# Two-layer hybrid trunk on one core: low halves of the activations in a plane of their own, ring slots of low weights at four start offsets

## The chip, the cores and the metric

The kernel runs on one core of a Trainium2 chip. The metric is the device time of one execution in microseconds, lower is better; a result is the median of several runs.

## What is computed

Two layers act on a residual stream x of 256 tokens by 1024 channels, in float32. Cut to what matters for the time:

```python
for l in range(DEPTH):                                   # DEPTH = 2
    mix = hybrid_mixer(x, w_in[l], ...)                  # one input projection, three mixers, merge, output projection
    x = layer_norm(ALPHA * x + mix, ln1_g[l], ln1_b[l])
    ffn = swiglu(x, w_ffn_gate[l], w_ffn_up[l], w_ffn_down[l])   # (silu(x @ w_gate) * (x @ w_up)) @ w_down, hidden 2816
    x = layer_norm(ALPHA * x + ffn, ln2_g[l], ln2_b[l])
```

The mixers are a sliding-window attention, a gated short convolution and a block attention (with 256 tokens, plain causal attention). Each is projected to 1024 channels, weighted by a sigmoid gate and summed. Nearly all arithmetic is the products of x, and of what is made from it, with weight matrices.

## The kernel before, in words

**Products in three parts.** Each float32 operand is split into a high half (rounded to the type `float32r`) and a low half (what the rounding left). A product is three matmuls: high by high, high by low, low by high. They come in trios from two helpers, both through `mm` on line 256, so that nearly all matmuls have that line:

```python
def trio(acc, wh, wl, src, first, last):         # weights stationary, 256 tokens moving
    mm(acc, wh, src[:, 0, :], first, False)
    mm(acc, wh, src[:, 1, :], False, False)
    mm(acc, wl, src[:, 0, :], False, last)
```

`tokens` does the same the other way round: 128 tokens are stationary and 256 or 512 columns of weights move. Of each matmul the weight load of the stationary operand is an instruction of its own (LDWEIGHTS). In a trio the order of stationary operands is wh, wh, wl and of moving ones high, low, high; in `tokens` the stationary ones are high, high, low and the moving ones wh, wl, wh.

**Weights.** The weights stand in DRAM as 140 pieces of 128 partitions by 2048 columns (70 for a layer), in the order of use. SyncE loads a piece into one of 3 `raw` tiles; ScalarE writes its high half `wh` (line 184) and VectorE its low half `wl` (line 185), in two chunks of 1024 columns. The halves go to the pool `wts`, which has four slots for `wh` and four for `wl`. Each slot is 2048 elements, 8192 bytes in a partition. The slots are used in turn, and `drop` frees one when its last matmul is issued. Three pieces of a layer go to other places, the halves of one tile `wA` or `wB`, and do not pass through the ring.

**Activations.** `xx` holds x transposed, as 8 blocks of 128 channels; of each block the 256 high halves come first and then the 256 low halves (index order k, a, s). 48 elements (`AHEAD`, 192 bytes) are left free ahead of it, and a filler tile `rest` of 16 elements brings the sum back to a multiple of 256 bytes. `y`, the results of the three mixers, has the same 48 elements ahead. `mx` (input of the output projection), `hidA` and `hidB` (the FFN's hidden values) have none.

**Stages, and which helper each uses.** For each layer: `whole` (tile `acc`, `trio` on `xx`) for the input projections, among which the attention rounds (`s`, `tp`, `yp`) are interleaved; `cv`, a product with 512 moving columns of weights; `branch` (tile `br`, `trio` on `y`); `merge` (tile `gc`, `trio` on `xx`); `project` (tile `pr`, `tokens` on `mx`, 512 moving columns); `half_pair` (tile `hp`, `tokens` on `xx`, 256 moving columns) for the first FFN pieces, and for the first input projections of each layer; `whole` again (tile `acc`) for the FFN's 18 remaining pieces; `project` on `hidA`, `hidB`, where the last layer has some blocks of 256 columns.

**The order of the work.** A planner (`Plan`) sets, while the program is built, the order on TensorE, VectorE, ScalarE and SyncE from costs that it holds; addresses play no part in it.

**Offsets before.** Start addresses here are bytes within a partition, modulo 256. Each slot of `wh` and `wl` starts at 0, and each stationary or moving block within it is a multiple of 512 bytes further, so all weights stand at 0. All blocks of `xx` and `y`, high and low, stand at 192; `mx`, `hidA` and `hidB` at 0.

Of the kernel before, what the change touches and what calls it, by code (L numbers as in the profile page):

```python
# [10 lines left out]
FR = mybir.dt.float32r  # L11
# [5 lines left out]
P = 128  # L17
D = 1024
S = 256
L = 2  # L20
KD = D // P
# [3 lines left out]
PIECE = 2048  # L25
# [7 lines left out]
LN_EPS = 1e-5  # L33
FAR = 1.0e30
LINE = 64
AHEAD = 48


# [77 lines left out]
def trunk(ctx: ExitStack, tc: tile.TileContext, x, xt, w, sinks, conv, ln, out):  # L116
# [4 lines left out]
    wts = pool("wts", RING)  # L121
    keep = pool("keep", 1)
# [13 lines left out]
    spare, ready, chunks, raw, landed, rawfree = {}, {}, {}, {}, {}, {}  # L136
# [6 lines left out]
    def load(ks=None):  # L143
        j = pos["load"]
        if j >= total:
            return
        pos["load"] += 1
        raw[j] = raws.tile([P, PIECE], FT, name="raw")
        if ks is None:
            for s in cut(j):  # L150
                nc.sync.dma_start(raw[j][:, s], w[j][:, s])
        else:
            a, b = by_k(raw[j]), by_k(w[j])
            for k in ks:
                nc.sync.dma_start(xs[:, k, :], xt[:, k, :])
                nc.sync.dma_start(a[:, :, k, :], b[:, :, k, :])  # L156
        landed[j] = max(landed.get(j - 1, 2.5), rawfree.get(j - RAWS, 0.0) + 2.0) + 3.0
        open_splits()
# [4 lines left out]
    def open_splits():  # L163
        while pos["split"] < pos["load"]:
            j = pos["split"]
            if j in place:
                if place[j] not in spare:
                    return
                t = spare.pop(place[j])
                both = keep.tile([P, 2, PIECE], FR, tag=place[j], name="w" + place[j])  # L170
                ready[j] = both[:, 0, :], both[:, 1, :]
            else:
                if not slots:
                    return
                t = slots.pop(0)
                ready[j] = wts.tile([P, PIECE], FR, name="wh"), wts.tile([P, PIECE], FR, name="wl")
            pos["split"] += 1
            if j:
                split_piece(j, max(t, landed[j]))
# [7 lines left out]
    def split_piece(j, t, n=CHUNK):  # L187
        def last(task):
            rawfree[j] = task.ready
            load()  # L190

        need = T.pe + 5.2 * (j - pos["take"])
        ss = [slice(c, c + n) for c in range(0, PIECE, n)]
        chunks[j] = [T.add(parts(j, s), t - (1.5 if len(cut(j)) > 1 and not i else 0.0), max(need - t, 0.0) + 0.001 * i, last if s.stop == PIECE else None)
                     for i, s in enumerate(ss)]

    def take():
        j = pos["take"]
        pos["take"] += 1
        T.run()  # L200
        T.finish(*chunks.pop(j))
        return j

    def drop(j):
        if j in place:
            if j % PER_LAYER == N_IN + N_BR + N_OUT:
                spare["B"] = T.pe
        else:
            slots.append(T.pe)
        del ready[j]  # L210
        open_splits()
# [90 lines left out]
        users.append(t)  # L302
        return t

    xx = keep.tile([P, AHEAD + KD * 2 * S], FR, name="xx")
    xx = xx[:, AHEAD:].rearrange("p (k a s) -> p k a s", k=KD, a=2)
    xk = [xx[:, k] for k in range(KD)]
    rest = keep.tile([P, LINE - AHEAD], FT, name="rest")
    nc.gpsimd.memset(rest, 0.0)
# [292 lines left out]
    def mixer_tiles():  # L602
        mix = keep.tile([P, 18 * S + 4 * (S + 2) + 56], FT, tag="mix", name="mix")
        aq, ak, av, cq, ck, cv = [
            mix[:, lo * S:hi * S].rearrange("p (k s) -> p k s", k=k)
            for lo, hi, k in ((0, 4, 4), (4, 5, 1), (5, 6, 2), (6, 10, 4), (10, 14, 4), (14, 18, 2))]
        return aq, ak[:, 0, :], av, cq, ck, cv, mix[:, 18 * S:18 * S + 4 * (S + 2)].rearrange("p (k s) -> p k s", k=4)
# [26 lines left out]
    for l in range(L):  # L634
        aq, ak, av, cq, ck, cv, up = tiles = mix or mixer_tiles()
        y = keep.tile([P, AHEAD + 12 * 2 * S], FR, tag="A", name="y")
        y = y[:, AHEAD:].rearrange("p (b k a s) -> p b k a s", b=3, k=4, a=2)
        nc.gpsimd.memset(up[:, :, 0:2], 0.0)
# [39 lines left out]
        for n in range(2):  # L678
            j = take()
# [50 lines left out]
        if l == 0:  # L730
            rest = keep.tile([P, LINE - AHEAD], FT, name="rest2")
            nc.gpsimd.memset(rest, 0.0)
# [70 lines left out]
        merge()  # L803
        spare["A"] = spare["B"] = T.pe
        open_splits()

        hid, last_f = [], {f: [] for f in range(NF)}
# [125 lines left out]
```

## Time and profile before

| | us |
|---|---|
| median of 3 runs | 862.95 (859.62 to 865.4) |
| the profiled execution | 860.16 |
| its span, first to last instruction | 858.4 |
| granted TensorE clock, mean over the span | 0.997 |
| TensorE matmuls busy | 844.8 (98%) |
| VectorE busy | 583.5 (68%) |
| ScalarE busy | 456.3 (53%) |

The span is 1.8 us shorter than the profiled execution's own time. A duration of a matmul in the profile is that of one instruction with its fill and drain, and successive matmuls overlap; how fast they follow one another is read from their starts.

### The profile page before, as it was taken

The page shows a single profiled execution, that of the slowest core. Times are in us where ns is not written, and L with a number is a line of the kernel's source. Part 1 is how long each engine was busy: PE and PEld are TensorE (multiplying, and loading weights), DVE is VectorE, ACT ScalarE, POOL GpSimd, SP SyncE. Part 2 cuts the span into 40 slices and gives each one's busy share as a digit, 9 for nine tenths or more (in the row PEclk, how much of TensorE's full clock was granted, in tenths as well). Part 3 has the DMA queues.
Part 4 walks back from the last instruction along what each step waited for, and adds up shares of the span by engine and source line. Part 5 has one row for each costly group of instructions (what it writes and reads, how often), then busy time and mean ns, then how long its engine had stood idle before and what let it go on. Part 6 is the DMA issues. An engine that isn't in the chain of part 4 may idle for free.

```text
span 858.4 us, 15516 instructions
## 1 busy us (share of the span) xinstructions
PE 844.8 (98%) x6374; PEld 797.3 (93%) x6374; DVE 583.5 (68%) x977; ACT 456.3 (53%) x809; POOL 51.4 (6%) x81
## 2 busy tenths in 40 slices
PE   7999999999999999999999999999999999999996
PEld 7989999999899999988899899999997999999885
DVE  5678888567976666545656798876689575666435
ACT  6667577745535445434337757776564254444320
POOL 2003400000100000000000034000000000000000
PEclk9999999999999999999999999999999999999998
DMA  8754535365755555556337352544557465555511
GB/s 300 289 195 150 187 108 186 140 216 176 265 197 180 174 187 197 196 189 238 119 116 255 116 196 99 186 138 169 196 197 254 139 245 187 173 185 193 196 50 49
DMA packets 24822, 155.16 MB, mean 181 GB/s; under 512 B 2704, under 2 KB 4528, under 8 KB 7344
## 3 DMA queue, kind: packets, MB, share of 16 engines
q1 hardware_dynamic: 23536, 149.96, 49.9%
q0 software_dynamic: 1216, 4.22, 1.5%
q8 instruction: 50, 0.82, 0.4%
q14 instruction: 20, 0.16, 0.1%
HBM read 153.11 MB, written 1.05 MB: 180 GB/s over the span
## 4 chain that ended last, share of the span: by engine, by line
PE 96%; DMA 2%; DVE 1%; ACT 0%; issue 0%; SPq 0%; POOLq 0%; POOL 0%; DVEq 0%
PE acc L256 47%; PE pr L256 17%; PE hp L256 9%; PE br L256 8%; PE gc L256 5%; PE s L256 3%; PE cv L256 3%; PE tp L271 2%; DMA gb<-ln 1%; PE yp L474 1%; DMA xs<-xt 1%; PE yp L476 0%; DVE xtok L502 0%; DVE wA L185 0%; SPq L156 0%
## 5 line engine op out<-in xcount | busy, mean ns | idle before, releaser
L256 PE MATMUL acc<-xx,wh 128*128 128x256 f32 x2304 | 408.9, 282 | 5.6 <-ACT wh L276 5.6
L185 DVE TENSOR_TENSOR wl<-raw,wh 128x1024 fp32r<-128x1024 f32 x266 | 321.9, 1228 | 123.2 <-ACT wh L184 122.3
L184 ACT ACTIVATE wh<-raw 128x1024 fp32r<-128x1024 f32 x266 | 273.5, 1054 | 188.5 <-PE acc L256 81.6
L256 PEld LDWEIGHTS acc<-xx,wh 128*128 128x128 f32 x2304 | 353.9, 190 | 6.7 <-ACT wh L276 6.2
L256 PE MATMUL acc<-xx,wl 128*128 128x256 f32 x1152 | 323.2, 281 | 0.0
L256 PEld LDWEIGHTS acc<-xx,wl 128*128 128x128 f32 x1152 | 217.7, 189 | 0.2 <-DVE wl L277 0.2
L256 PE MATMUL hp<-wh,xx 128*128 128x256 f32 x384 | 70.5, 281 | 0.0
L283 DVE TENSOR_TENSOR g<-g,acc 128x256 f32<-128x256 f32 x72 | 30.1, 417 | 58.7 <-PE acc L256 58.7
L256 PE MATMUL br<-y,wh 128*128 128x256 f32 x384 | 67.9, 281 | 0.0
L256 PE MATMUL pr<-wh,hidA 128*128 128x512 f32 (+1 forms) x216 | 60.8, 366 | 0.0
L256 PEld LDWEIGHTS hp<-wh,xx 128*128 128x128 f32 x384 | 59.5, 188 | 0.0
L256 PEld LDWEIGHTS br<-y,wh 128*128 128x128 f32 x384 | 59.0, 190 | 0.0
L256 PE MATMUL br<-y,wl 128*128 128x256 f32 x192 | 54.0, 281 | 0.0
L256 PE MATMUL hp<-wl,xx 128*128 128x256 f32 x192 | 53.5, 279 | 0.0
L256 PE MATMUL gc<-xx,wh 128*128 128x256 f32 x256 | 45.3, 281 | 0.0
L256 PEld LDWEIGHTS pr<-wh,hidA 128*128 128x128 f32 x216 | 39.1, 189 | 6.7
L256 PE MATMUL pr<-wh,hidB 128*128 128x512 f32 (+1 forms) x144 | 41.8, 366 | 0.0
L256 PE MATMUL pr<-wl,hidA 128*128 128x512 f32 (+1 forms) x108 | 39.6, 366 | 0.0
L256 PEld LDWEIGHTS gc<-xx,wh 128*128 128x128 f32 x256 | 39.3, 190 | 0.0
L429 ACT ACTIVATE prob<-prob,st 128x128 f32<-128x128 f32 x32 | 12.6, 395 | 46.3 <-DVE st L426 23.3
L256 PEld LDWEIGHTS hp<-wl,xx 128*128 128x128 f32 x192 | 36.1, 188 | 0.0
L256 PEld LDWEIGHTS br<-y,wl 128*128 128x128 f32 x192 | 36.0, 188 | 0.0
(130 smaller groups left out, 982.0 us busy)
## 6 DMA issues: line engine op xcount, KB each, us to landing
raw<-w SPq DMA_DIRECT2D x136, 1024.0 KB, 4.9
gb<-ln POOLq DMA_DIRECT2D x8, 512.0 KB, 5.9
raw<-w SPq DMA_DIRECT2D x6, 512.0 KB, 6.5
xtok<-x SPq DMA_DIRECT2D x2, 512.0 KB, 6.3
xs<-xt SPq DMA_DIRECT2D x3, 256.0 KB, 5.4
raw<-w SPq DMA_DIRECT2D x3, 256.0 KB, 5.5
out<-xtok SPq DMA_DIRECT2D x3, 256.0 KB, 2.0
xs<-xt SPq DMA_DIRECT2D x2, 128.0 KB, 2.5
```

The lines of the kernel that those rows point to most:

```text
L184: return [act(n) + (lambda: nc.scalar.activation(wh[:, s], raw[j][:, s], AF.Copy),), dve(n) + (lambda: nc.vector.tensor_sub(wl[:, s], raw[ ...
L185: dve(n) + (lambda: nc.vector.tensor_sub(wl[:, s], raw[j][:, s], wh[:, s].bitcast(FT)),)]
L256: nc.tensor.matmul(acc, a, b, start=start, stop=stop)
L271: nc.tensor.transpose(tp[:, i, :], src(i), ident)
L283: return [dve(n) + (lambda: nc.vector.tensor_mul(dst, a, b),)]
L429: nc.scalar.activation(t[:, 0, :], t[:, 0, :], AF.Exp, bias=st[:, 2:3], scale=0.125, accum_out=st[:, 4:5])
L474: nc.tensor.matmul(yp[los[a], :], v[:, 0, vsel[a]], pts[a][:, 0:2, :], start=True, stop=False)
```

## The change

`xx` is laid out as two planes: first all high halves (8 blocks of 256), then all low halves. Between the planes 32 elements (`APART`, 128 bytes) are left free, and as many after the second, so that the tile stays a multiple of 256 bytes with `AHEAD` and `rest`. The high halves stay at 192 modulo 256; the low ones stand at 192 + 8192 + 128, which is 64 modulo 256.

Each slot for low weights gets 16 elements more than are used (64 bytes), so that the four slots, which lie one after the other, start at 0, 64, 128 and 192 modulo 256. The slots for high weights, `wA`, `wB`, `y`, `mx` and the hidden values stay where they were modulo 256.

```diff
+APART = 32
...
-                ready[j] = wts.tile([P, PIECE], FR, name="wh"), wts.tile([P, PIECE], FR, name="wl")
+                ready[j] = (wts.tile([P, PIECE], FR, name="wh"),
+                            wts.tile([P, PIECE + 16], FR, name="wl")[:, :PIECE])
...
-    xx = keep.tile([P, AHEAD + KD * 2 * S], FR, name="xx")
-    xx = xx[:, AHEAD:].rearrange("p (k a s) -> p k a s", k=KD, a=2)
+    xx = keep.tile([P, AHEAD + 2 * (KD * S + APART)], FR, name="xx")
+    xx = xx[:, AHEAD:].rearrange("p (a r) -> p a r", a=2)[:, :, :KD * S].rearrange("p a (k s) -> p k a s", k=KD)
```

No instruction is added, removed or moved: each engine has the same instructions with the same waits in the same order. Three splits of `xs` at the start, on ScalarE and VectorE each, now write one run of 512 elements where they wrote two of 256.

## Rows read from the trace of the kernel before

**Rows 1.** The page, part 1: busy us (share) and count of instructions.

```profile
PE 844.8 (98%) x6374; PEld 797.3 (93%) x6374; DVE 583.5 (68%) x977; ACT 456.3 (53%) x809; POOL 51.4 (6%) x81
```

**Rows 2.** The page, part 4: shares of the chain that ended last, by engine.

```profile
PE 96%; DMA 2%; DVE 1%; ACT 0%; issue 0%; SPq 0%; POOLq 0%; POOL 0%; DVEq 0%
```

**Rows 3.** The chain in order of time: start us, us, engine, tile, line, matmuls.

```profile
3.09 4.51 DMA xs<-xt
...
21.22 8.16 PE hp L256 x72
...
76.24 8.18 PE acc L256 x72
...
90.29 8.48 PE acc L256 x72
...
162.61 33.92 PE br L256 x288
196.53 22.61 PE gc L256 x192
...
269.16 98.94 PE acc L256 x840
...
428.99 8.48 PE hp L256 x72
```

**Rows 4.** TensorE in time, slow rhythm: start us, us, engine, line, operation.

```profile
303.86 0.28 PE L256 MATMUL acc<-xx,wl 128*128 128x256 f32 x1
...
303.98 0.40 PE L256 MATMUL acc<-xx,wh 128*128 128x256 f32 x2
...
304.10 0.19 PEld L256 LDWEIGHTS acc<-xx,wl 128*128 128x128 f32 x1
304.22 0.28 PE L256 MATMUL acc<-xx,wl 128*128 128x256 f32 x1
```

**Rows 5.** TensorE in time, last projection, blocks of 256 columns.

```profile
848.75 0.88 PE L256 MATMUL pr<-wB,hidB 128*128 128x256 f32 x6
849.47 0.28 PE L256 MATMUL pr<-wh,hidB 128*128 128x256 f32 x1
```

**Rows 6.** TensorE in time, eight transposes in a row.

```profile
250.28 1.03 PE L271 MATMUL tp<-ident,xtok 128*128 128x128 f32 x8
251.15 0.38 PE L271 MATMUL tp<-ident,gh 128*128 128x128 f32 x2
```

**Rows 7.** TensorE in time, 512 moving columns: the tile cv, then the tile pr.

```profile
50.81 0.39 PE L256 MATMUL cv<-wl,xx 128*128 128x512 f32 x1
...
52.87 0.39 PE L256 MATMUL cv<-wl,xx 128*128 128x512 f32 x1
...
370.25 0.39 PE L256 MATMUL pr<-wl,hidA 128*128 128x512 f32 x1
...
371.61 0.39 PE L256 MATMUL pr<-wl,hidA 128*128 128x512 f32 x1
```

**Rows 8.** Groups by line, different shapes apart: busy us, mean ns, idle before.

```profile
L256 PE MATMUL acc<-xx,wl 128*128 128x256 f32 x1152 | 323.2, 281 | 0.0
L185 DVE TENSOR_TENSOR wl<-raw,wh 128x1024 fp32r<-128x1024 f32 x266 | 321.9, 1228 | 123.2 <-ACT wh L184 122.3
...
L256 PE MATMUL gc<-xx,wl 128*128 128x256 f32 x128 | 36.0, 281 | 0.0
...
L256 PE MATMUL pr<-wl,hidA 128*128 128x512 f32 x84 | 32.8, 390 | 0.0
...
L256 PE MATMUL pr<-wl,hidB 128*128 128x512 f32 x56 | 21.8, 390 | 0.0
...
L256 PE MATMUL pr<-wl,mx 128*128 128x512 f32 x48 | 18.7, 390 | 0.0
```

**Rows 9.** Stretches: us, PE busy (count), granted clock, DMA share, GB/s.

```profile
34.00:40.00 6.00, 6.00 (x55) 1.00 0.86 300
...
285.00:355.00 70.00, 70.00 (x597) 1.00 0.53 185
```

## The prediction

> **What bounds the kernel now.** I read the page first, then the chain, then TensorE's starts. The page shows matmuls busy for 98% of the span [rows 1], and the chain that ended last runs through TensorE for 96% [rows 2], so the time is what its 6,374 matmuls take one after the other. Busy time cannot tell whether they run at their best, since a busy 281 ns [rows 8] is a matmul with its fill and drain. How close they follow shows in the chain, which gives a piece's length and its count of matmuls [rows 3]. The reader is to see that the same work has two paces: 72 matmuls of the tile acc take 8.18 us in one piece (113.6 ns each) and 8.48 us in the next (117.8 ns). The clock does not differ: it is granted in full in a stretch of either kind [rows 9]. In the slow FFN piece of 840 matmuls the mean is 98.94 / 840 = 117.8 ns, so the pace holds for a hundred microseconds.
>
> Adding up the chain's pieces of acc, hp, br and gc by their pace gives 3,624 matmuls at 117 ns and above: in each of the two layers 840 of the FFN, 288 br and 192 gc [rows 3], 2,640 together, and 984 in pieces of 24 to 72, as the hp piece at 428.99 and the acc piece at 90.29. The other 1,416 with 256 columns are at 113 to 114 ns, all in the mixers' part of the two layers; 5,040 in all.
>
> **What addresses have to do with it.** The weight load of the next matmul begins with the matmul now running [rows 4]: the load of wl at 304.10 starts beside the second wh matmul, the one that moves the low activations. So each matmul has a moving operand and a load that read SBUF at the same time. I call their difference of start addresses, moving less stationary, modulo 256 bytes, the offset of the pair. Before, the offset is 192 for all of acc, gc and br and 64 for all of hp. The rows with other offsets:
> - Offset 0, 256 columns (last projection): six matmuls start in 849.47 - 848.75 = 0.72 us, 120.0 ns each [rows 5].
> - Offset 192: 113.6 or 117.8 ns. Offset 64 (hp): 8.16 / 72 = 113.3 or 8.48 / 72 = 117.8 ns [rows 3].
> - Offset 128: only transposes, which move 128 columns: eight in 251.15 - 250.28 = 0.87 us, 108.8 ns each [rows 6]. Half as many moving columns make this a lower bound and not a price.
> - 512 columns: offset 64 (cv) nine in 2.06 us, 229 ns; offset 0 (pr) six in 1.36 us, 227 ns [rows 7].
>
> So the offset is worth some ns for a matmul, but the same offset has two paces, and once a pace is taken it lasts until something interrupts it. Which one is taken after an interruption differs between two attention rounds of the same form (the pieces at 76.24 and 90.29) [rows 3].
>
> **The change, part by part.** It moves no instruction, so only durations and paces can change. The sum is made against the profiled execution's 860.16 us; the median of the runs is 862.95, 2.8 us above it, and the same difference is applied to that.
>
> *The low plane and the low slots.* In a trio two pairs keep their offset of 192 (high activations beside wh). The third, low activations (64) beside wl at 0, 64, 128 or 192, gets 64, 0, 192 or 128 in place of 192, a quarter of the pieces each. What this does to the pace no row shows. Bounds: every one of the 5,040 at 120.0 (3,624 x 2.2 + 1,416 x 6.4 ns = +17.0 us), every one at 108.8 (3,624 x 9.0 + 1,416 x 4.8 ns = -39.4 us). I take the value that the fast pieces show, 113.6, for the stages whose moving operand is `xx` or whose stationary operand is: the slow pace needs three equal pairs in a row for as long as 840 matmuls, and now one in three differs and differs anew with each piece of weights. This is where I choose, and it is the weakest step. For br I take nothing, as `y` does not move. Then 3,624 - 576 = 3,048 matmuls gain 117.8 - 113.6 = 4.2 ns: -12.8 us.
>
> *The quarters that do worse or better.* acc and gc have 1,152 + 128 = 1,280 matmuls with wl, one for each low pair [rows 8], 320 for each slot. The slot at 64 gives offset 0, 120.0 in place of 113.6: 320 x 6.4 ns = +2.0 us. The slot at 192 gives offset 128, taken at the bound of 108.8: 320 x 4.8 = -1.5 us. In hp (offsets of wl moving against low activations) and br the two cancel within 0.4 us. Sum: -12.8 + 2.0 - 1.5 = -12.3 us.
>
> *Projections.* Of pr's matmuls with 512 columns, 84 + 56 + 48 = 188 move low weights of the ring [rows 8], and three quarters of them change offset. Between 227 and 229 ns that is 188 x 0.75 x 2 ns = 0.3 us either way; I take nothing.
>
> *Splits.* VectorE writes wl at other addresses, 266 chunks of 1,228 ns [rows 8]. It has 123 us of waiting for ScalarE before them, so a few ns more in each would be covered. The three longer runs at the start replace as many elements; the start waits for loads (4.51 us in the first piece of the chain) [rows 3]. Both at nothing.
>
> *What comes late next.* With 12 us less on TensorE nothing else is near: VectorE is busy 68%, ScalarE 53% [rows 1], and the FFN moves 185 GB/s where another stretch moved 300 [rows 9].
>
> Forecast: 862.95 - 12.3 = 850.6, said as 851 us.
>
> **A rule against the change.** The rows give 113.6, 117.8 and 120.0 ns to matmuls of one shape, [rows 3, 5], and the first two differ at the same full clock [rows 9]. The Trainium skill, page "TensorE: Matmul & The Clock Gate", section "Step-by-step: what each phase is for", says of the two read ports: "Loading the next tile's weights doesn't steal SBUF read bandwidth from the running matmul." By that rule the offsets mean nothing and the result is 863. The trace does not bear it out, since the matmuls at offset 0 are slower than any at 192; but those belong to another tile, so it is not refuted either, and it stands below as the first rival.
>
> **The rivals.**
> - *Offsets mean nothing* (863). The paces come from elsewhere, and the change touches nothing that counts. For it: the paces change where attention interrupts, with no change of address [rows 3]. Against it: 120.0 at offset 0 [rows 5].
> - *Gains and losses cancel* (859, 855 to 871). The two pairs at 192 keep their pace, and only the third changes. For it: one offset has both paces, so the offset does not decide alone, and with the middle of the two paces, 115.7, for offsets 64 and 192, the four slots have a mean of (115.7 + 120.0 + 115.7 + 108.8) / 4 = 115.1 against 117.8, 2.7 ns on one matmul in three or 5,040 / 3 x 2.7 = 4.5 us. Against it: the slow pace would have to outlive a change of every third pair.
> - *The new offsets bring on the slow pace* (872). A new slot every 48 matmuls is an interruption, and after it the slow pace is taken, as after the round before 90.29. The 1,416 fast matmuls then lose 4.2 ns, +5.9 us; in the quarter with offset 0 the trio as a whole falls to 120.0, 5,040 / 4 x 2.2 = +2.8 us; and the projections lose what cv has over pr, +0.3. Sum +9.0: 872.0. It decides once the 1,416 are lost and one slot drags its trio. For it: at offset 0 every matmul of the row takes 120. Against it: before the interruptions mostly lead into the fast pace (the pieces with 8.18).
> - *More than forecast* (840). br follows as well, all 3,624 gain 4.2 ns (-15.2), and low pairs go to 108.8 in every trio, 5,040 / 3 x 4.8 = -8.1.
>
> **How the numbers follow.** Forecast 0.40, offsets mean nothing 0.10, cancel 0.22, slow pace 0.20, more 0.08. That the change does not do what it says is left out: the sizes of the tiles fix the addresses. Faster by over 1% (under 854.3; 1% is about what a measurement of this kernel tells from no change) takes the forecast and more, 0.48; same 0.32; slower (over 871.6) 0.20. Range: 840 below and the slow rival above with its edge, 838 to 874. The forecast's own range is 845 to 856.
>
> **What would show it.** In the chain after: FFN pieces at 113 to 114 ns a matmul (95.6 us for 840) say the forecast; 98.9 us says nothing moved; over 100 us the slow rival. The pace piece by piece should repeat every four pieces of weights if slots decide. br at 33.9 us for 288 says `y` is untouched. It would be wrong if the pace stayed even over all four slots.

## The result, and the profile after

| | before | after |
|---|---|---|
| median of 20 runs, us | 862.15 (859.62 to 866.96) | 868.91 (866.48 to 873.28) |
| the profiled execution, its span, us | 860.16, 858.4 | 869.29, 867.5 |

The ratio is 1.0085, with a 95% interval of 1.0073 to 1.0098: the change makes the kernel 0.85% slower, 6.8 us. Forecast were 851 us, with a range of 838 to 874. The range holds the result, but the sign of the forecast was wrong.

The page after, parts 1 and 4, beside [rows 1, 2]:

```profile
PE 851.8 (98%) x6374; PEld 801.3 (92%) x6374; DVE 585.6 (68%) x977; ACT 457.0 (53%) x809; POOL 50.9 (6%) x81
PE 95%; DMA 2%; DVE 1%; SPq 1%; issue 0%; ACT 0%; POOLq 0%; POOL 0%; DVEq 0%
```

The counts are the same, and TensorE is still the chain. Matmul busy time rose by 7.0 us; where it was lost the page cannot say. The chain in order of time can. After (start us, us, engine, tile, line, matmuls):

```profile
6.81 7.68 DMA raw<-w
...
22.67 8.51 PE hp L258 x72
...
79.02 8.57 PE acc L258 x72
...
93.56 8.57 PE acc L258 x72
...
167.40 33.11 PE br L258 x288
200.51 22.75 PE gc L258 x192
...
273.51 99.51 PE acc L258 x840
373.02 56.58 PE pr L258 x246
...
434.63 8.39 PE hp L258 x72
...
504.00 8.43 PE acc L258 x72
...
592.42 33.39 PE br L258 x288
...
699.51 99.58 PE acc L258 x840
799.09 61.13 PE pr L258 x330
```

And the chain before at those places that [rows 3] leave out:

```profile
368.10 55.80 PE pr L256 x246
...
583.75 33.92 PE br L256 x288
...
691.20 98.94 PE acc L256 x840
790.14 60.95 PE pr L256 x330
```

The starts of the same stage in both give an account of the 9.1 us between the two profiled executions (the medians lie 6.8 us apart; the execution profiled before was 2 us under its median):

| stretch | lost, us |
|---|---|
| up to the first hp piece (21.22, then 22.67) | 1.45 |
| mixers of the first layer, up to br (162.61, then 167.40: 4.79 - 1.45) | 3.34 |
| br and gc, first layer (33.92 + 22.61, then 33.11 + 22.75) | -0.67 |
| projection and hp, up to the FFN (269.16, then 273.51) | 0.23 |
| FFN, first layer (98.94, then 99.51) | 0.57 |
| projections, up to hp (428.99, then 434.63) | 0.72 |
| mixers of the second layer, up to br (583.75, then 592.42) | 3.03 |
| br to the FFN, second layer (691.20, then 699.51) | -0.36 |
| FFN, second layer (98.94, then 99.58) | 0.64 |
| the rest | 0.18 |

The first row is the landing of the first loads and has nothing to do with the change: in the profiled executions of the kernels below, where the chain has that hp piece, it starts anywhere between 20.98 and 23.35. Of the other 7.7 us, 6.4 are lost in the mixers. There [rows 3] have pieces of 72 in 8.18 and 8.48 us; after, no piece of 72 in acc is under 8.43. The fast pace is gone. br, which the forecast held untouched, gained 0.5 to 0.8 us.

The pace of acc after repeats every four pieces of weights; in time the slots come in the order 128, 0, 192, 64. The clock is granted in full (1.00 from 285 to 355 us). TensorE in time, first layer's FFN, the matmuls with wl, one for each trio: the end of a piece in the slot at 192, then the slot at 64 (start us, us, engine, line, operation):

```profile
307.36 0.29 PE L258 MATMUL acc<-xx,wl 128*128 128x256 f32 x1
...
309.88 0.29 PE L258 MATMUL acc<-xx,wl 128*128 128x256 f32 x1
...
311.30 0.28 PE L258 MATMUL acc<-xx,wl 128*128 128x256 f32 x1
...
313.38 0.28 PE L258 MATMUL acc<-xx,wl 128*128 128x256 f32 x1
```

From 307.36 to 309.88 there are seven trios: 2.52 us / 21 = 120.0 ns a matmul. From 311.30 to 313.38 there are six: 2.08 / 18 = 115.6 ns. The same means over all parts of 24 matmuls of that FFN, split by the pair (mean ns from one start to the next in the trace, without the first six and the last of each part, good to about 1 ns; in brackets the offset of the pair):

| slot | high by wh | low by wh | high by wl | mean |
|---|---|---|---|---|
| 0 | 116.2 (192) | 119.6 (64) | 117.4 (192) | 117.7 |
| 64 | 113.6 (192) | 118.4 (0) | 115.0 (192) | 115.7 |
| 128 | 119.0 (192) | 122.5 (192) | 120.3 (192) | 120.6 |
| 192 | 121.4 (192) | 115.1 (128) | 123.4 (192) | 120.0 |

The reader is to see two things. The low pair's own offset counts for some ns, as forecast. But the first pair, whose addresses modulo 256 are the same in all four rows, takes 113.6 to 121.4 ns: a pair cannot be priced alone. The mean of the four slots is 118.5, above the slow pace of before.

### The profile page after: what moved, and what is told of

Read it like the earlier page. It is cut to its first block, busy times and chain, and to the rows that moved or that the text cites. A ratio compares the mean times of both kernels' runs of the same rounds, so it can differ in the third digit from the quotient of the medians.

```text
span 867.5 us, 15516 instructions
## 1 busy us (share of the span) xinstructions
PE 851.8 (98%) x6374; PEld 801.3 (92%) x6374; DVE 585.6 (68%) x977; ACT 457.0 (53%) x809; POOL 50.9 (6%) x81
## 4 chain that ended last, share of the span: by engine, by line
PE 95%; DMA 2%; DVE 1%; SPq 1%; issue 0%; ACT 0%; POOLq 0%; POOL 0%; DVEq 0%
PE acc L258 47%; PE pr L258 17%; PE hp L258 9%; PE br L258 8%; PE gc L258 5%; PE s L258 3%; PE cv L258 3%; PE tp L273 2%; DMA gb<-ln 1%; PE yp L476 1%; DMA raw<-w 1%; PE yp L478 0%; SPq L157 0%; SPq L156 0%; DVE xtok L504 0%
## 5 line engine op out<-in xcount | busy, mean ns | idle before, releaser
L258 PE MATMUL acc<-xx,wh 128*128 128x256 f32 x2304 | 415.0, 283 | 6.2 <-ACT wh L278 6.1
L258 PE MATMUL gc<-xx,wl 128*128 128x256 f32 x128 | 36.1, 282 | 0.0
```

Of the source, the lines that this page charges most:

```text
L258: nc.tensor.matmul(acc, a, b, start=start, stop=stop)
```

## The experiments

Two theories were set against each other. *Addresses set the pace*: the start addresses of the trio's operands as a whole give its pace, slot by slot. *Rotation*: a change of slot every 48 matmuls is an interruption that breaks a pace or brings it on, as forecast and slow rival had it. A third, that the layout in planes counts by itself, stood beside the first four runs. Ratios are to the kernel before on the same chip.

**The plane alone** (slots all at 0).

```diff
+APART = 32
...
-    xx = keep.tile([P, AHEAD + KD * 2 * S], FR, name="xx")
-    xx = xx[:, AHEAD:].rearrange("p (k a s) -> p k a s", k=KD, a=2)
+    xx = keep.tile([P, AHEAD + 2 * (KD * S + APART)], FR, name="xx")
+    xx = xx[:, AHEAD:].rearrange("p (a r) -> p a r", a=2)[:, :, :KD * S].rearrange("p a (k s) -> p k a s", k=KD)
```

> The change's shifted low plane alone; all slots of low weights start at 0 as before. Addresses set the pace (theory): each combination of offsets has its own pace, and the slot at 0 with the shifted plane had 117.7 ns a matmul in every piece of the changed kernel. So all acc pieces run at 117.7: the FFN's 840 stay at 98.9 us, the attention pieces of 72 take 8.48 and none takes 8.18; 1,416 x 4.2 ns = +6 us, 868 us. Rotation of slots breaks the fast pace (rival): without rotation the pieces of 8.18 come back, 862 us.

Measured: 863.38 us, ratio 0.9998 (0.9979 to 1.0017). The chain:

```profile
78.63 8.48 PE acc L257 x72
...
166.65 32.65 PE br L257 x288
...
245.40 8.17 PE hp L257 x72
...
272.42 98.94 PE acc L257 x840
```

The time is the same within the interval, and yet two things moved against each other. All twelve acc pieces of 72 take 8.48 us: the shifted plane takes the fast pace away with no slot rotating. br came into the fast pace (32.65 / 288 = 113.4 ns) though `y`, `wh` and `wl` stand where they stood before, and three of the four hp pieces of 72 take 8.17 where before they took 8.48. Summed over the chain without the first piece of each tile, acc takes 5.1 us more, br 2.6 and hp 0.8 us less; the 1.7 us that remain lie at the edge of the interval. The forecast of 868 had the acc pieces right and missed br and hp, so that by its time alone this run would have spoken for the wrong theory.

**The slots alone** (activations unmoved).

```diff
-                ready[j] = wts.tile([P, PIECE], FR, name="wh"), wts.tile([P, PIECE], FR, name="wl")
+                ready[j] = (wts.tile([P, PIECE], FR, name="wh"),
+                            wts.tile([P, PIECE + 16], FR, name="wl")[:, :PIECE])
```

> The slots at 0, 64, 128 and 192 alone; the activations lie as before. Addresses: all stages behave as br did in the changed kernel, where the activations had not moved: 113.3 for the slots at 0 and 128, 117.8 to 118.2 for those at 64 and 192, a mean of 115.7; 840 FFN matmuls in 97.2 us, and over all 3,624 x -2.1 + 1,416 x +2.1 ns = -4.6 us, with about +1.5 in the projections: 859 us. Rotation: the fast pieces are lost, 840 in 98.9 us or more, 868 us.

Measured: 858.89 us, ratio 0.9965 (0.9951 to 0.9980).

```profile
270.63 97.11 PE acc L257 x840
...
498.27 8.49 PE acc L257 x72
...
512.66 8.18 PE acc L257 x72
```

Rotation alone costs nothing in the sum: the time is 0.35% less. The fast pace stands, in the slots at 0 and 128 (113.3 ns from the starts in the first FFN), and the slots at 64 and 192 take 118.1 and 117.8. The mean of the four, 115.6, is the FFN's 97.11 / 840. In the mixers, where most pieces were fast before, the same slots cost something: the twelve acc pieces of 72 have a mean of 8.36 us against 8.28.

**Planes without the shift** (the first diff with `APART = 0`).

> Two planes, but no 128 bytes between them, and slots at 0: every block of xx stands at 192 as before, only its order in the tile differs (the low block 8 KB further on and not 1 KB). Addresses modulo 256 set the pace: as before, 862 us, with pieces of 72 at 8.18 and at 8.48 and the FFN at 98.9. Layout (rival: the distance of the two halves counts): 866 us or more, the 8.18 gone.

Measured: 861.7 us, ratio 0.9996 (0.9985 to 1.0006).

```profile
76.91 8.18 PE acc L257 x72
...
90.96 8.48 PE acc L257 x72
...
271.02 98.94 PE acc L257 x840
```

The pieces of 8.18 and 8.48 us are there as before, and so are br's 33.92 and the FFN's 98.94. The layout by itself does nothing; the 128 bytes do.

**Slots at 0, 128, 0, 128** (activations unmoved; the slots' diff with `PIECE + 32`).

> Activations as before, slots of low weights at 0 and 128 in turn. Addresses: br ran at 113.3 with just these two slots, and entered that pace in the slot at 128; so acc, gc and br run at 113.3 to 113.6 throughout, 840 FFN matmuls in 95.3 us, 3,624 x -4.2 ns = -15 us, 847 to 849 us. Rotation: two slots in turn break the fast pace as four do, 862 to 868 us.

Measured: 852.44 us, ratio 0.9885 (0.9862 to 0.9908).

```profile
78.75 8.20 PE acc L257 x72
...
164.98 32.64 PE br L257 x288
...
269.41 95.54 PE acc L257 x840
364.96 56.29 PE pr L257 x246
...
508.86 8.48 PE acc L257 x72
```

Both stages of the forecast's gain are there: 95.54 / 840 = 113.7 ns in the FFN, 113.3 in br. It came out 3 to 5 us above what was expected. The sum had given the fast pace to 576 slow matmuls of hp too, which stay at 117.8 ns (2.4 us); slot 0 still falls back to 8.48 us after an attention round; and the projections lose 0.5 us in the piece of 246.

The start of the FFN shows what a change of slot does. TensorE in time, matmuls with wl (start us, us, engine, line, operation):

```profile
269.49 0.28 PE L257 MATMUL acc<-xx,wl 128*128 128x256 f32 x1
...
277.98 0.28 PE L257 MATMUL acc<-xx,wl 128*128 128x256 f32 x1
...
288.86 0.28 PE L257 MATMUL acc<-xx,wl 128*128 128x256 f32 x1
...
299.74 0.28 PE L257 MATMUL acc<-xx,wl 128*128 128x256 f32 x1
```

The slots at 0 and 128 come in pairs here. Up to 277.98 the slots at 0 take 8.49 us / 72 = 117.9 ns a matmul; up to 288.86 those at 128 take 10.88 / 96 = 113.3; up to 299.74 those at 0 again take 113.3. So the pace at 0 depends on what ran before it, and after a slot at 128 it is the fast one; with the slots alone, too, the slot at 0 comes right after the one at 128. In that much rotation was right: a change of slot can end a slow pace.

From the changed kernel and these four runs the pace of each slot was known, and the next three were forecast from it.

**All slots at 128** (activations unmoved).

```diff
-    wts = pool("wts", RING)
+    whs = pool("whs", RING)
+    gap = pool("gap", 1).tile([P, 32], FT, name="gap")
+    wls = pool("wls", RING)
+    gap2 = pool("gap2", 1).tile([P, 32], FT, name="gap2")
+    nc.gpsimd.memset(gap, 0.0)
+    nc.gpsimd.memset(gap2, 0.0)
...
-                ready[j] = wts.tile([P, PIECE], FR, name="wh"), wts.tile([P, PIECE], FR, name="wl")
+                ready[j] = whs.tile([P, PIECE], FR, name="wh"), wls.tile([P, PIECE], FR, name="wl")
```

> Activations unmoved, all four slots for low weights at 128. Addresses set the pace: each piece of 72 keeps or enters 113.3 ns (8.16 to 8.20 us), the FFN's 840 take 95.2, br 32.6, the 512-column projections with slot 128 lose about 3 ns each: 850 to 852 us, no slower than slots 0 and 128 in turn. Rotation (a change of slot breaks a slow pace): nothing rotates, so the pieces of 8.48 us and the 98.9 us are back: 862 us.

Measured: 850.6 us (849.83 to 855.22), ratio 0.9886 (0.9864 to 0.9907).

```profile
77.81 8.21 PE acc L261 x72
...
163.87 32.64 PE br L261 x288
196.51 21.76 PE gc L261 x192
...
268.57 95.21 PE acc L261 x840
363.79 57.22 PE pr L261 x246
...
640.38 12.03 DMA gb<-ln
```

Nothing rotates, and acc, gc and br are at 113.3 to 114 ns in every piece of 72 and more behind the first: the rotation theory, which said 862, falls. All twelve acc pieces of 72 are between 8.18 and 8.21 us. The profiled execution itself took 855.22; its wait for `ln` was 12.03 us where before it was 9.55.

**The shifted plane with all slots at 64** (the first diff and the last one, with fillers of 16 and 48 elements).

> Low activations shifted as in the change, all slots at 64. Addresses set the pace: 115.6 ns in every acc and gc part, so pieces of 72 in 8.32 us, 840 in 97.1 us, gc 22.2, br all at 118.2 (34.0 us): about 860 us. Rotation: without it the kernel is the one with shifted planes and fixed slots, pieces of 8.48 and 98.9 us, 863 us.

Measured: 860.78 us, ratio 0.9988 (0.9976 to 0.9999).

```profile
76.79 8.33 PE acc L262 x72
...
163.56 34.04 PE br L262 x288
...
270.04 97.09 PE acc L262 x840
```

**The shifted plane with all slots at 128** (the same with fillers of 32 and 32).

> Low activations shifted as in the change, all slots at 128. Addresses set the pace: 120.6 ns in every acc and gc part (3,800 matmuls, 2.1 ns over the mean of the four slots, +8 us), pieces of 72 in 8.68 us, 840 in 101.3 us, br all at 113.3 (32.6 us, -1): about 876 us, slower than the change though no slot rotates. Rotation: fixed slots, so 863 us as with all slots at 0.

Measured: 876.25 us, ratio 1.0170 (1.0157 to 1.0184).

```profile
78.72 8.70 PE acc L262 x72
...
168.40 32.68 PE br L262 x288
...
274.59 101.55 PE acc L262 x840
```

Both came out within 1 us of the sums made from addresses (860 and 876), piece by piece. The second is slower than the change itself although no slot rotates in it, and it differs from the kernel of 850.6 only in the planes of `xx` with the 128 bytes between them, of which the planes by themselves did nothing (with all slots at 0): 101.55 against 95.21 us for the same 840 matmuls. VectorE and ScalarE write the halves of the weights to the same offsets in these two, so their writes are not the difference. And the two kernels of the shifted plane, with all slots at 64 and at 128, differ by 64 bytes of filler alone: 97.09 and 101.55 us. The clock is not the cause. Stretches of the kernel with 101.55 and of that with 95.21, inside the FFN (us, busy and count by engine, granted clock, DMA share, GB/s):

```profile
285.00:355.00 70.00, 70.00 (x581) 70.00 (x580) 41.89 (x61) 32.83 (x49) 0.00 (x0) 1.00 0.55 183
```

```profile
280.00:350.00 70.00, 70.00 (x620) 70.00 (x619) 44.17 (x66) 34.76 (x51) 0.00 (x0) 1.00 0.58 196
```

The clock is granted in full in both, and 581 matmuls stand against 620 in the same 70 us.

**The projections' stationary operand** (all slots at 128, and `mx`, `hidA`, `hidB` moved by 128 bytes; then by 64, with 16 for 32).

```diff
+    def held(tag, name, k):
+        t = keep.tile([P, 32 + k * 2 * S], FR, tag=tag, name=name)
+        return t[:, 32:].rearrange("p (k a s) -> p k a s", k=k, a=2)
...
-        mx = keep.tile([P, KD, 2, S], FR, tag="mix", name="mx")
+        mx = held("mix", "mx", KD)
...
-                    hid.append(keep.tile([P, F_A, 2, S], FR, tag="A", name="hidA"))
+                    hid.append(held("A", "hidA", F_A))
...
-        hid.append(keep.tile([P, NF - F_A, 2, S], FR, tag="mix", name="hidB"))
+        hid.append(held("mix", "hidB", NF - F_A))
```

> As the kernel with all slots at 128, and mx and the hidden values start at 128 instead of 0, so that only the projections' stationary operand moves. Addresses set the pace also with 512 columns: pr's pieces change (the two of 246 and 330 matmuls took 57.2 and 61.0 us) by some ns of 230 a matmul, up or down, which no row tells; everything else stays: 843 to 857 us. Rival, the stationary operand of a matmul with 512 columns does not matter: 57.2 and 61.0 us, 851.

> The same with mx and the hidden values at 64. Addresses: pr's pieces differ from 57.2 and 61.0 us and from those with 128: 843 to 857 us. Rival: 57.2 and 61.0 us, 851.

Measured: 850.96 us, ratio 0.9877 (0.9855 to 0.9899), and 851.0 us, ratio 0.9867 (0.9848 to 0.9887). The chain of the first, then of the second:

```profile
363.92 56.37 PE pr L261 x246
...
780.49 61.03 PE pr L261 x330
```

```profile
363.33 56.89 PE pr L261 x246
...
782.94 61.33 PE pr L261 x330
```

The piece of 330 stays within 0.4 us of 61.0. The piece of 246 takes 0.85 us less with 128 and 0.33 less with 64, which is 3.5 and 1.3 ns a matmul. The starts of its matmuls with 512 columns on weights of the ring show more (mean ns from one start to the next in the trace, in the order of the trio; wl at 128):

| hidden values at | high by wh | high by wl | low by wh | mean |
|---|---|---|---|---|
| 0 | 235.0 | 234.0 | 229.6 | 232.9 |
| 128 | 232.6 | 225.8 | 228.4 | 228.9 |
| 64 | 231.4 | 229.0 | 233.0 | 231.1 |

So the rival does not hold for the pace: the address of the stationary operand counts with 512 columns too, by 2 to 8 ns for a pair. In the time of the kernel it does not show (850.6, 850.96 and 851.0 us).

## Why the prediction was wrong

- *What bounds the kernel*: right. What was lost after the first loads, and what the kernel with all slots at 128 gains (in the first layer 3.7 us in the FFN, 1.3 in br, 0.9 in gc), is TensorE's own rhythm at a full clock; VectorE and ScalarE play no part.
- *The failed step* is the one called the weakest: the pace of 113.6 for every stage on `xx`, because "the slow pace needs three equal pairs in a row". It does not. With the plane shifted, the pairs of the trio are never three equal ones in the slots at 0, 64 and 192, and no slot reaches 113.6 in the mean: 117.7, 115.7, 120.6 and 120.0. The slot at 128 has three pairs of offset 192 again, the offset of the trios that took 113.6 or 117.8 before, and is the slowest. So neither equality nor the difference of the two addresses sets the pace. Of the term of -12.8 us each FFN was to have 840 x 4.2 = 3.5 us and gc 0.8; measured are losses of 0.6 and 0.1, and in the mixers the fast pace was lost where a gain was said. The term also held 576 slow matmuls of hp, 2.4 us; hp gained 0.5 behind its first piece.
- *The quarters*: offset 0 was taken at 120.0 and measures 118.4, within 2 ns; offset 128, taken at its bound of 108.8, measures 115.1, so the gain of 1.5 us was not there. The trios were priced wrongly altogether. But the slot that gives offset 0 is the best of the four, and the one that gives offset 128 is among the worst, since the other two pairs of the trio move the other way. Rows of another tile [rows 5, 6] gave a pair's price without its neighbours.
- *br*: taken at nothing, it gained 0.8 and 0.5 us. The change puts three quarters of its wl at other slots: in the kernels with one slot throughout, br takes 32.6 us at 128 and 34.0 at 64. The forecast reasoned from `y`, which does not move, and let the moved wl of br cancel within 0.4 us. Part of the gain can also be the second pace of the slot at 0: with the plane alone br took it with no address of its own moved.
- *Projections*: 0.3 us either way was said, from 227 to 229 ns; the two large pieces lost 0.8 and 0.2. The span was too narrow: with wl at 128 and the hidden values at 0 the matmuls with wl take 234.0 ns. Splits and waits: nothing, as said.
- *The slow rival* (872, chance 0.20) had the size and the place: the mixers lost 3.3 us in the first layer and 3.0 in the second by the account above, where 5.9 in all was said for the fast matmuls there. Its reason was wrong, and that its sum came near is in part luck. A change of slot is no interruption that costs: with the slots alone the fast pace stays in two of the four slots, with the plane alone it goes. And its 2.8 us for the slot with offset 0, whose trio was to fall to 120.0, are the slot that came out best (115.7).
- *Offsets mean nothing* (863) is refuted by 850.6 against 876.25 for kernels that differ in the layout of one tile. The Trainium skill, page "TensorE: Matmul & The Clock Gate", section "Step-by-step: what each phase is for", says that the weight load of the next tile takes no read bandwidth from the running matmul. These runs show that the pace depends on where operands start; that it is the load and the moving read that disturb each other was assumed here, and no run shows it.

The three sums made from the paces by slot (850 to 852, 860 and 876) came within 1 us. What the forecast lacked were rows: none showed a trio with unequal addresses, the better of the two paces seen at other addresses was taken for it, and the reason given for that, equal pairs in a row, stood in no row.

Two things stay open. Why one set of addresses (activations at 192, all weights at 0) has two paces is not explained; it keeps the one it has until the work or the slot changes. And which property of the three addresses sets the pace is not known; the measured combinations are all there is. The start of wh and of the high activations was not varied in a trio with 256 columns.

## What to carry to other kernels

When matmuls follow one another without idle time at a full clock and still take 4% more in one stage than in another, try the start addresses of their operands: a filler of 128 bytes ahead of the pool of low weights was worth 1.1% here, and the same 128 bytes in the other operand's tile as well cost 1.7%. Price such a change by the whole repeating group of matmuls, with a run for each combination, never by one pair. And read the pieces of the chain even when the time is unchanged: the plane alone showed no difference clear of noise, as a gain in br and hp stood against a larger loss in acc.

## What was not expected of the hardware

- The pace of a trio with 256 columns by its start addresses (high activations at 192, wh at 0), from the chain's pieces of 840: 113.3 ns (low activations at 192, wl at 128), 115.6 (64 and 64), 117.8 (64 and 0), 120.9 (64 and 128).
- In one kernel, a pair with the same two addresses modulo 256 takes 113.6 to 121.4 ns as the other operands of the trio move.
- With 512 columns the same holds for a pair: 225.8 to 234.0 ns for the matmul with wl as the stationary operand's start goes from 128 to 0.
- With low activations at 192 and wl at 128 every piece of 72 is at the fast pace (8.18 to 8.21 us); with both the same but wl at 0, some are and some are not (8.18 and 8.48 [rows 3]). There a pace lasts, 840 matmuls long at 117.8 ns, and a slot at 128 before it brings the fast one (117.9, then 113.3).
